# RMSNorm sums as four 32-column products, roots on 128 partitions, and a spread by row-picking products, in a two-layer diffusion backbone

## The chip, the cores and the metric

One core of one Trainium2 chip runs the whole program. TensorE (PE) multiplies, VectorE (DVE), ScalarE (ACT) and GpSimd (POOL) work on elements, and SyncE (SP) starts the DMAs. Each engine takes its own instructions in order and waits on semaphores for the others. The metric is device microseconds of one execution, as the median over runs.

## The reference, cut to what matters

Two layers over 512 latent tokens of width 1024 with 256 context tokens: layer 0 mixes tokens by multi-head latent attention, layer 1 by a Hyena long convolution, and a gated ConvFFN follows each. Every sub-layer begins with an RMS norm and a modulation. The change touches only how the norms are computed:

```python
def rmsnorm(x, g):
    y = x * lax.rsqrt(jnp.mean(x * x, axis=-1, keepdims=True) + EPS)
    return y * g

hx = modulate(rmsnorm(x, norm_mix_g[i]), sh1, sc1)          # also on the context in layer 0
cq = rmsnorm(h @ w_dq, g_q)                                 # width 512
ckv = rmsnorm(kv[..., :KV_LORA], g_kv)                      # width 256
x = x + g1 * mixer(hx)
x = x + g2 * conv_ffn(modulate(rmsnorm(x, norm_ffn_g[i]), sh2, sc2))
return rmsnorm(x, final_g)
```

## The kernel before, in words

Activations lie with the width on partitions and tokens along the free dimension, so the sum over the width is a sum over partitions, and it is made on TensorE. The weights of the large products are split in a high and a low part (`wh`, cast on ACT, L137; `wl`, a subtraction on DVE, L138), and so are the activations (`hxh`/`hxl`, `hf0h`/`hf0l`, `hf1h`/`hf1l`, ...): a product is three matmuls. All matmuls are issued through one helper, so they share line L68.

A norm (class `Norm`, L240 to L304) goes through these steps. Chunk by chunk of 128 channels, ACT squares into `sqa` (the first chunk) or into `sq` (L273), and POOL adds `sq` into `sqa` (L275); the last chunk is squared on DVE into its own `sq` (L280). `colsum` multiplies `sqa` and the last `sq` with a column of ones: 128 tokens of squares are the stationary operand, the moving operand has one column, and the sums land in `cols`, one token per partition, one column for each 128 tokens. `finish` takes the reciprocal root on DVE by a bit trick and three Newton steps (11 instructions on `rsq`, 128 partitions by 2, 4 or 6 columns), makes diagonal matrices `dg` (the identity times a column of roots, L301), and a product of `ones` with `dg` spreads the roots over all partitions (`bc`, `bcc`, `bk`, `bq` in PSUM). `modulated` (L312) then scales on DVE (`hx`, L314), casts on ACT (`...h`, L315) and subtracts on DVE (`...l`, L316).

Norms stand in these places, in order of time: the latent input (4 blocks of 128 tokens, `x`), whose squares are made during the filter phase; the context input (2 blocks, `xc`); `nk` (6 blocks, width 256, spread into `bk`); `nq` (4 blocks, width 512, spread into `bq`); then four norms in two halves of 256 tokens each: before the first FFN (`hf0`), before Hyena (`hy`), before the second FFN (`hf1`) and the final one.

The filter phase (before 73 us) makes the Hyena filters: TensorE makes `fps`, DVE multiplies by a window into `ff` (the window `win` is from ACT), ACT and POOL or DVE split `ff` into `pqh` and `pql`, TensorE transforms these to `fa`, `fb`, `fo`, and DVE evaluates (`fee`, `fev`, `fs`). Between these products stand those of the modulation vectors (class `Mods`): `modp` is four products of 32 stationary columns each that fill four quarters of the PSUM partitions, ACT copies it to `ev` (in the tag "sq"), `modq` transposes it, DVE adds the bias into `modc`. After layer 0's start the modulation is summed on DVE instead (`macc`, L227).

The order on each engine comes from a list scheduler that places every instruction by its dependences and its free buffers; buffers come from pools in which a tag has a fixed number (`bufs`) that are reused in turn. The tag "sq" has two.

Of the kernel before, what the change touches and what calls it, by code (L numbers as in the profile page):

```python
# [44 lines left out]
    VOFF[_n] = (_o, _w)  # L45
    _o += _w
NV = _o
CST = [("ident", 128), ("perm", 128), ("tneg", 4), ("sgn", 1)]
COFF = {}
_o = 0  # L50
for _n, _w in CST:
    COFF[_n] = (_o, _w)
    _o += _w
NCST = _o


@with_exitstack
def hybrid_kernel(ctx, tc, A, out):
# [35 lines left out]
        psum[:] = [stack.enter_context(tc.tile_pool(name=name, bufs=1, space=PSUM, reuse_waits="tile")), n, o]  # L94

    vec = gp.tile([P, NV], F32, name="vec")
    cst = gp.tile([P, NCST], F32, name="cst")
    dma(out=cst, in_=A["cst"])
    dma(out=vec, in_=A["vec"])

    def V(name, a=0, b=None):
# [3 lines left out]
    def K(name):  # L105
        o, w = COFF[name]
        return cst[:, o:o + w]
# [2 lines left out]
    ident_r = gp.tile([P, P], F32R, name="ident_r")  # L110
    perm_r = gp.tile([P, P], F32R, name="perm_r")
    nc.vector.tensor_copy(out=ident_r, in_=ident)
    nc.vector.tensor_copy(out=perm_r, in_=K("perm"))
    ones = gp.tile([P, P], F32, name="ones")
    nc.gpsimd.memset(ones, 1.0)
    modc = gp.tile([P, 2, 48, 2], F32, name="modc")
    gsc = gp.tile([P, 5, 8], F32, name="gsc")
    hcc = gp.tile([P, 3, 24], F32, name="hcc")
    sc = gp.tile([P, 8, 32], F32, name="sc")
    nc.gpsimd.memset(sc, 0.0)  # L120
    act(out=sc[:, :, 0], in_=V("c"), func=AF.Silu)
    act(out=sc[:, :, 1], in_=V("cctx"), func=AF.Silu)

    fspec = dr.tile([4, 2, P, 2, 2, 256], F32, name="fspec")
    xspill = dr.tile([P, NC, T], F32, name="xspill")
# [33 lines left out]
    class Mods:  # L159
# [31 lines left out]
        def step_pe(self, n, ws, pool, ahead=0):  # L191
            for _ in range(min(n, len(self.todo))):
                l, u, n, k = self.todo.pop(0)
                self.rows(sc[:, k, :], ws.pop(0), n, k == 0, k == NC - 1)
                if k == NC - 1:
                    self.columns(l, u, n, 2, pool)
                if ahead and len(self.todo) >= ahead:
                    ws.append(self.load(self.todo[ahead - 1], pool, "mw", ahead))
# [15 lines left out]
        def step(self, n, pool, bufs, after):  # L214
            self.age += 1
            self.finish()
            if self.age > 1:
                self.flush()
            for _ in range(min(n, len(self.todo))):
                k0 = self.todo.pop(0)  # L220
                l, u, n, k = k0
                w = self.load(k0, pool, "mw", bufs)
                if k == 0:
                    self.acc = pool.tile([P, 2048], F32, tag="macc", name="macc", bufs=2)[:, :n * 1024]
                    i = vts(out=self.acc, in0=w, scalar1=sc[:, k, 0:1], scalar2=None, op0=ALU.mult)
                else:
                    i = stt(out=self.acc, in0=w, scalar=sc[:, k, 0:1], in1=self.acc, op0=ALU.mult, op1=ALU.add)  # L227
                in_order(after, i)
                if k == NC - 1:
                    self.due = (self.acc, l, u, n, pool)  # L230
                    self.age = 0
# [8 lines left out]
    class Norm:  # L240
        def __init__(self, n, nt, dim, tmp, halves=1):
# [4 lines left out]
            self.due, self.n_add = [], 0  # L246
            self.cols = [pso("cols") for _ in range(halves)]

        def flush(self, lag=0):
            while self.due and self.due[0][0] <= self.n_add - lag:  # L250
                self.colsum(*self.due.pop(0)[1:])

        def colsum(self, src, h, first, last):
            for t in range(self.nth):
                m = mm(self.cols[h][:, t:t + 1], lhsT=src[:, t * P:(t + 1) * P], rhs=ones[:, 0:1],
                       start=first and t == 0, stop=last and t == self.nth - 1)
                self.last[h] = in_order(self.last[h], m)

        def add(self, xj, h=None):
            self.n_add += 1  # L260
            self.flush(self.nh)
            n, w = self.n, self.nth * P
            hs = list(range(self.nh)) if h is None else [h]
            j = self.j[hs[0]]
            for i in hs:
                self.j[i] += 1
            if j == 0 and n > 2:
                self.acc = self.tmp.tile([P, self.nt * P], F32, tag="sqa", name="sqa", bufs=1)
                act(out=self.acc, in_=xj, func=AF.Square)
                return  # L270
            sq = self.tmp.tile([P, self.nt * P], F32, tag="sq", name="sq", bufs=2)[:, :w * len(hs)]
            if j < n - 1 and n > 2:
                act(out=sq, in_=xj, func=AF.Square)  # L273
                acc = self.acc[:, hs[0] * w:hs[-1] * w + w]
                nc.gpsimd.tensor_tensor(out=acc, in0=acc, in1=sq, op=ALU.add)  # L275
                if j == n - 2:
                    for i in hs:
                        self.due.append((self.n_add, self.acc[:, i * w:(i + 1) * w], i, True, False))
                return
            vtt(out=sq, in0=xj, in1=xj, op=ALU.mult)  # L280
            for i, q in enumerate(hs):
                self.due.append((self.n_add, sq[:, i * w:(i + 1) * w], q, j == 0, j == n - 1))

        def finish(self, bc, h=0, after=None, mm_after=None):
            if mm_after is not None:
                self.last = [mm_after] * self.nh
            self.flush()
            nt, tmp = self.nth, self.tmp
            v = tmp.tile([P, 3, 8], F32, tag="rsq", name="rsq", bufs=2)
            vv, y, t_ = v[:, 0, :nt], v[:, 1, :nt], v[:, 2, :nt]  # L290
            in_order(after, vts(out=vv, in0=self.cols[h][:, :nt], scalar1=1.0 / self.dim, scalar2=EPS, op0=ALU.mult,
                                op1=ALU.add))
            vts(out=y.bitcast(I32), in0=vv.bitcast(I32), scalar1=-0.5, scalar2=float(0x5F3759DF), op0=ALU.mult,
                op1=ALU.add)
            for _ in range(3):
                stt(out=t_, in0=y, scalar=-0.5, in1=y, op0=ALU.mult, op1=ALU.mult)
                vtt(out=t_, in0=t_, in1=vv, op=ALU.mult)
                stt(out=y, in0=t_, scalar=1.5, in1=y, op0=ALU.add, op1=ALU.mult)
            dg = tmp.tile([P, self.nt * P], F32, tag="sq", name="dg", bufs=2)
            for t in range(nt):  # L300
                vts(out=dg[:, t * P:(t + 1) * P], in0=ident, scalar1=y[:, t:t + 1], scalar2=None, op0=ALU.mult)  # L301
            n = nt * P // len(bc)
            for i, b in enumerate(bc):
                in_order(mm_after, mm(b, lhsT=ones, rhs=dg[:, i * n:(i + 1) * n], start=True, stop=True))  # L304

    def rstd_bc(chunks, nt, dim, tmp, bc, after=None):
        nm = Norm(len(chunks), nt, dim, tmp)
# [168 lines left out]
    def mla():  # L476
        L = {}
        with ExitStack() as st:
            a1 = st.enter_context(tc.tile_pool(name="a1", bufs=1, side="left"))
            x = a1.tile([P, NC, T], F32, tag="x", name="x")  # L480
            xc = a1.tile([P, NC, TC], F32, tag="xc", name="xc")
            psum_pool(st, "pa", 5)
            mods = Mods([(0, 0, 2), (0, 2, 2)])

# [10 lines left out]
            def first_loads():  # L495
                ws.extend(mods.load(mods.todo[k], *slots[k]) for k in range(NE, 4))
                for i in range(4):
                    dma(out=x[:, 2 * i:2 * i + 2, :], in_=A["x"][:, 2 * i:2 * i + 2, :])
                ws.extend(mods.load(mods.todo[k], *slots[k]) for k in range(4, 8))
                dma(out=xc, in_=A["ctx"])  # L500

            nm = Norm(NC, 4, D, a1)
            hooks, started, wk = [], [], []
# [34 lines left out]
    def latents(step, nm, nrm, a1, a2, x, xc, L):  # L538
# [15 lines left out]
        for rh, rl, n, o in ((hh, hl, T, TC), (ch, cl, TC, 0)):  # L554
# [10 lines left out]
            else:  # L565
                nc.scalar.copy(out=kpe[64:96, :TC], in_=pss[2][64:96, :n])
            step(2)
        nk = Norm(2, 6, 256, nrm)

        def norm_kv(m):  # L570
# [7 lines left out]
        for b in range(2):  # L578
            w = split_w(A["wdq"][b], 2048)
            w = (wcols(w[0], 8, 256), wcols(w[1], 8, 256))  # L580
            pss = [pst(f"dq{i}") for i in range(2)]
            gemm([(pss[0], *w, 0), (pss[1], *w, P)], lambda k: hh[:, k, :], lambda k: hl[:, k, :], 8,
                 halfway=norm_kv if b else None)
            for i in range(2):
                nc.scalar.copy(out=cq[:, 2 * b + i, :], in_=pss[i])
            if b == 0:
                for j in range(2):
                    nk.add(ckv[:, j, :])
            step(2)
        L["wuk"] = split_w(A["wuk"], 2048)  # L590
        wr = wp.tile([P, 2048], F32, tag="wr", name="wr", bufs=3)
# [24 lines left out]
        nq = Norm(4, 4, 512, nrm)  # L616
        for j in range(4):
            nq.add(cq[:, j, :])
        kb = L["kb"]
        kh, kl = kb[0]  # L620
        nc.scalar.copy(out=kh[64:96], in_=kpe[64:96])
        nc.gpsimd.tensor_tensor(out=kl[64:96], in0=kpe[64:96], in1=kh[64:96], op=ALU.subtract)
# [501 lines left out]
    psum_pool(ctx, "pc", 5)  # L1124
    with tc.tile_pool(name="f0", bufs=1, side="left", reuse_waits="tile") as fp:
        x = fp.tile([P, NC, T], F32, name="x0")
        dma(out=x, in_=A["x"])
        mods = Mods([(0, 4, 1)])
        th = ToH(x, Norm(NC, 4, D, fp, 2), 2, 0, 3, fp, "hf0")
# [14 lines left out]
    yh, yl = hyena(hh, hl)  # L1144
    with tc.tile_pool(name="f1", bufs=1, side="left", reuse_waits="tile") as fp:
        x = fp.tile([P, NC, T], F32, name="x1")
        for i in range(4):
            dma(out=x[:, 2 * i:2 * i + 2, :], in_=xspill[:, 2 * i:2 * i + 2, :])
        th = ToH(x, Norm(NC, 4, D, fp, 2), 3, 1, 3, fp, "hf1")
# [145 lines left out]
```

## Time and profile before

| | |
|---|---|
| time, median of 3 runs | 1453.72 us (1452.2 to 1455.11) |
| the profiled execution | 1458.08 us, its span 1456.3 us |
| TensorE | 1385.1 us busy, 95% of the span |
| VectorE | 959.1 us, 66% |
| ScalarE | 562.2 us, 39% |
| GpSimd | 224.2 us, 15% |
| TensorE clock granted, mean | 0.984 of full |

The span is the time between the first and the last instruction that the profiler saw; the execution's own time has 1.8 us more around it. A group of matmuls ends in the profile where its last modelled end lies, so that neighbouring rows overlap; the distance from start to start is what a piece of work takes.

### The profile page before, as it was taken

Reading aid. Unit: us, or ns where it says so; the run is one execution under the profiler, and the core shown is the slowest. Engines: PE = TensorE matmul, PEld = TensorE weight load, DVE = VectorE, ACT = ScalarE, POOL = GpSimd, SP = SyncE. Lnnn points to the kernel's source line nnn. Section 1 sums busy time; section 2 is a strip of 40 time slices with the busy share of each in tenths; the row PEclk is TensorE's granted clock in tenths of the full one; section 3 lists DMA queues with packets and bytes.
Section 4 is the critical chain, followed back from the end, with each engine's and each line's share of the span. In section 5 each row is a group of like instructions: output and inputs, shape, how many; then the busy total and the mean of one; then the engine's idle time right before and its main releaser. Section 6 shows DMA issues by size and latency. Waiting matters only on the chain. (4 is left out here: it accounts for less than half of the span.)

```text
span 1456.3 us, 17263 instructions
## 1 busy us (share of the span) xinstructions
PE 1385.1 (95%) x6702; PEld 1093.2 (75%) x6702; DVE 959.1 (66%) x1493; ACT 562.2 (39%) x853; POOL 224.2 (15%) x188
## 2 busy tenths in 40 slices
PE   5899899999999999999999999999999999999997
PEld 2577765656588878787878987887798888888886
DVE  6875665567377877567774688988776653355545
ACT  5444454546434433123432343323334432234421
POOL 4401054335330000000001103331300000000011
PEclk9999999999998999999999999999999999999998
DMA  9672511113262754765523442222313222332121
GB/s 372 215 270 98 145 41 48 43 64 115 80 232 85 240 174 151 260 228 174 183 70 137 141 164 88 87 87 68 136 59 116 78 74 100 115 112 78 60 80 59
DMA packets 46670, 186.58 MB, mean 128 GB/s; under 512 B 5320, under 2 KB 17864, under 8 KB 32380
## 3 DMA queue, kind: packets, MB, share of 16 engines
q1 hardware_dynamic: 46588, 185.48, 36.7%
q8 instruction: 53, 0.87, 0.2%
q14 instruction: 29, 0.24, 0.0%
HBM read 171.29 MB, written 11.60 MB: 126 GB/s over the span
## 5 line engine op out<-in xcount | busy, mean ns | idle before, releaser
L137 ACT CAST wh<-wr 128x1024 fp32r<-128x1024 f32 (+2 forms) x209 | 195.1, 955 | 190.2 <-PE dn L68 89.0
L138 DVE TENSOR_TENSOR wl<-wr,wh 128x1024 fp32r<-128x1024 f32 (+2 forms) x209 | 246.7, 1196 | 26.4 <-ACT wh L137 24.0
L275 POOL TENSOR_TENSOR sqa<-sqa,sq 128x512 f32<-128x512 f32 (+1 forms) x42 | 57.2, 1361 | 845.8 <-ACT sq L273 844.9
L68 PE MATMUL dn<-gh,wh 128*128 128x512 f32 (+1 forms) x396 | 147.5, 374 | 0.0
L68 PE MATMUL dn<-gl,wh 128*128 128x512 f32 (+1 forms) x396 | 146.4, 370 | 0.0
L68 PE MATMUL dn<-gh,wl 128*128 128x512 f32 (+1 forms) x396 | 146.2, 369 | 0.0
L326 DVE SCALAR_TENSOR_TENSOR z<-ua,vec,z 128x511 f32<-128x511 f32 x44 | 33.0, 750 | 111.3 <-ACT z L325 111.2
L954 DVE SCALAR_TENSOR_TENSOR x<-dn,modc,x 128x512 f32<-128x512 f32 (+1 forms) x36 | 24.9, 691 | 109.1 <-PE dn L68 109.1
L325 ACT ACTIVATE z<-ua,vec 128x512 f32<-128x512 f32 x44 | 34.2, 778 | 150.6 <-PE ua L68 150.6
L68 PEld LDWEIGHTS dn<-gh,wh 128*128 128x128 f32 x396 | 74.4, 188 | 15.6 <-ACT wh L137 0.8
L68 PEld LDWEIGHTS dn<-gh,wl 128*128 128x128 f32 x396 | 74.5, 188 | 14.3
L68 PEld LDWEIGHTS dn<-gl,wh 128*128 128x128 f32 x396 | 74.4, 188 | 13.9
L68 PE MATMUL hz<-hyh,wh 128*128 128x512 f32 (+1 forms) x224 | 82.2, 368 | 0.0
L68 PE MATMUL hz<-hyh,wl 128*128 128x512 f32 (+1 forms) x224 | 81.9, 367 | 0.0
L761 POOL TENSOR_TENSOR acc<-acc,pf 128x512 f32<-128x512 f32 x60 | 76.7, 1299 | 33.1 <-ACT pf L751 32.2
L68 PE MATMUL hz<-hyl,wh 128*128 128x512 f32 (+1 forms) x224 | 81.7, 366 | 0.0
L751 ACT ACTIVATE pf<-s 128x512 f32<-128x512 f32 x96 | 56.9, 596 | 47.6 <-PE s L68 45.2
L68 PE MATMUL ua<-hf1h,wh 128*128 128x512 f32 (+1 forms) x192 | 72.8, 379 | 1.1 <-ACT hf1h L315 1.1
L68 PE MATMUL ua<-hf0h,wh 128*128 128x512 f32 (+1 forms) x192 | 73.5, 383 | 0.0
L68 PE MATMUL ua<-hf1l,wh 128*128 128x512 f32 (+1 forms) x192 | 73.0, 380 | 0.5 <-DVE hf1l L316 0.5
L68 PE MATMUL ua<-hf0l,wh 128*128 128x512 f32 (+1 forms) x192 | 73.2, 381 | 0.0
L68 PE MATMUL ug<-hf0l,wh 128*128 128x512 f32 (+1 forms) x192 | 73.2, 381 | 0.0
(380 smaller groups left out, 3382.6 us busy)
## 6 DMA issues: line engine op xcount, KB each, us to landing
wr<-in_wup SPq DMA_DIRECT2D x44, 1024.0 KB
mw<-in_modw SPq DMA_DIRECT2D x40, 1024.0 KB
wr<-in_wdn SPq DMA_DIRECT2D x32, 704.0 KB
wr<-in_win SPq DMA_DIRECT2D x12, 1024.0 KB
mw<-in_modw SPq DMA_DIRECT2D x16, 512.0 KB
fspec<-fs SPq DMA_DIRECT2D x16, 256.0 KB
wr<-in_wo SPq DMA_DIRECT2D x4, 1024.0 KB
fq<-fspec SPq DMA_DIRECT2D x8, 512.0 KB
```

The lines of the kernel that those rows point to most:

```text
L68: i = nc.tensor.matmul(*args, **kw)
L137: nc.scalar.copy(out=wh[:, c], in_=wr[:, c])
L138: vtt(out=wl[:, c], in0=wr[:, c], in1=wh[:, c], op=ALU.subtract)
L275: nc.gpsimd.tensor_tensor(out=acc, in0=acc, in1=sq, op=ALU.add)
L325: act(out=z, in_=p, func=AF.Identity, bias=b, scale=w1)
L326: stt(out=z[:, 1:T], in0=p[:, 0:T - 1], scalar=w0, in1=z[:, 1:T], op0=ALU.mult, op1=ALU.add)
L751: act(out=pf, in_=s, func=AF.Exp, scale=ATT_SCALE)
L761: add(out=accs[h], in0=prev, in1=pf, op=ALU.add)
L954: i = stt(out=x[:, q, c], in0=job[0][:, c], scalar=mcol(l, 5, q), in1=x[:, q, c], op0=ALU.mult, op1=ALU.add)
```

## The change

Ones become the stationary operand, 32 columns of them, and the squares stream past. A norm of 4 blocks has its 512 tokens in four quarters of 128; each quarter's product goes to its own 32 PSUM partitions, where the sums stand in 32 equal rows. (A half of 256 tokens has quarters of 64, the context 64, `nk` 192.) So the 11 instructions of the root run on all 128 partitions by 64, 128 or 192 columns. There is no `dg`; instead, `pick[:, g, :]`, a matrix with one row of ones at partition 32g, is the stationary operand of four products that spread quarter g's roots over all partitions. `rsq` moves from a tag of its own into the tag "sq". The squares of `nk` are two tiles, and their sums are issued as soon as the tokens' part is there. The permutation matrix `perm` leaves the block of constants, is loaded on its own after the context into a tile of tag "sq", and is cast on POOL instead of DVE. `pick` is set on POOL in three pools; the vector for the modulation products moves.

```diff
     cst = gp.tile([P, NCP], F32, name="cst")
-    dma(out=cst, in_=A["cst"])
+    dma(out=cst, in_=A["cst"][:, :NCP])
...
-    nc.vector.tensor_copy(out=perm_r, in_=K("perm"))
-    ones = gp.tile([P, P], F32, name="ones")
+    ones = gp.tile([P, 64], F32, name="ones")
     nc.gpsimd.memset(ones, 1.0)
+    pick = {}
+
+    def make_pick(pool):
+        t = pick[0] = pool.tile([P, 4, P], F32, name="pick")
+        nc.gpsimd.memset(t, 0.0)
+        for g in range(4):
+            nc.gpsimd.memset(t[32 * g:32 * g + 1, g, :], 1.0)
...
+        def square(self, name):
+            return self.tmp.tile([P, min(self.nt, 4) * P], F32, tag="sq", name=name, bufs=2)
...
         def colsum(self, src, h, first, last):
-            for t in range(self.nth):
-                m = mm(self.cols[h][:, t:t + 1], lhsT=src[:, t * P:(t + 1) * P], rhs=ones[:, 0:1],
-                       start=first and t == 0, stop=last and t == self.nth - 1)
+            w = self.nth * 32
+            for g in range(4):
+                q = src[g // 2][:, g % 2 * w:(g % 2 + 1) * w] if isinstance(src, list) else src[:, g * w:(g + 1) * w]
+                m = mm(self.cols[h][32 * g:32 * g + 32, :w], lhsT=ones[:, 0:32], rhs=q,
+                       start=first, stop=last)
                 self.last[h] = in_order(self.last[h], m)
...
-            nt, tmp = self.nth, self.tmp
-            v = tmp.tile([P, 3, 8], F32, tag="rsq", name="rsq", bufs=2)
-            vv, y, t_ = v[:, 0, :nt], v[:, 1, :nt], v[:, 2, :nt]
-            in_order(after, vts(out=vv, in0=self.cols[h][:, :nt], scalar1=1.0 / self.dim, scalar2=EPS, op0=ALU.mult,
+            w = self.nth * 32
+            v = self.square("rsq")
+            vv, y = v[:, :w], v[:, w:2 * w]
+            t_ = v[:, 2 * w:3 * w] if w <= P else self.square("rsq2")[:, :w]
+            in_order(after, vts(out=vv, in0=self.cols[h][:, :w], scalar1=1.0 / self.dim, scalar2=EPS, op0=ALU.mult,
                                 op1=ALU.add))
...
-            dg = tmp.tile([P, self.nt * P], F32, tag="sq", name="dg", bufs=2)
-            for t in range(nt):
-                vts(out=dg[:, t * P:(t + 1) * P], in0=ident, scalar1=y[:, t:t + 1], scalar2=None, op0=ALU.mult)
-            n = nt * P // len(bc)
-            for i, b in enumerate(bc):
-                in_order(mm_after, mm(b, lhsT=ones, rhs=dg[:, i * n:(i + 1) * n], start=True, stop=True))
+            n = 4 // len(bc)
+            for g in range(4):
+                b = bc[g // n][:, (g % n) * w:(g % n + 1) * w]
+                in_order(mm_after, mm(b, lhsT=pick[0][:, g, :], rhs=y, start=True, stop=True))
...
                 dma(out=xc, in_=A["ctx"])
+                perm = a1.tile([P, T], F32, tag="sq", name="perm", bufs=2)[:, :P]
+                dma(out=perm, in_=A["cst"][:, NCP:])
+                nc.gpsimd.tensor_copy(out=perm_r, in_=perm)
...
                 for j in range(2):
                     nk.add(ckv[:, j, :])
+                nk.flush()
             step(2)
```

The change also moves instructions on every engine. On ACT in the filter phase, from the first square of the latent input `x` on, before:

```order
L269 ACTIVATE sqa<-x 128x512
L440 CAST pqh<-ff 128x512
L273 ACTIVATE sq<-x 128x512
L433 ACTIVATE win<-dec,cst 128x512
...
L273 ACTIVATE sq<-x 128x512 x2
...
L453 ACTIVATE fee<-fa 128x512
L273 ACTIVATE sq<-x 128x512 x2
L433 ACTIVATE win<-dec,cst 128x512
L440 CAST pqh<-ff 128x512 x2
L433 ACTIVATE win<-dec,cst 128x512
L440 CAST pqh<-ff 128x512 x2
L433 ACTIVATE win<-dec,cst 128x512
L181 COPY ev<-modp 128x512
```

And now, from the same place to the same copy:

```order
L279 ACTIVATE sqa<-x 128x512
...
L470 ACTIVATE fee<-fa 128x512
L457 CAST pqh<-ff 128x512 x2
L450 ACTIVATE win<-dec,cst 128x512
L457 CAST pqh<-ff 128x512 x2
L450 ACTIVATE win<-dec,cst 128x512
L291 ACTIVATE sq<-x 128x512 x6
L186 COPY ev<-modp 128x512
```

The six squares that POOL adds have moved from among the casts to behind the last of these windows and right ahead of `ev`. POOL's six additions move with them, behind all six of its `pql` in this stretch, with the cast of `perm` after the second; the buffers of the first three squares are one and the same, since `perm` holds the other of the tag "sq".

On PE in the second part of the filter phase, before (`hs_...` are the hidden layer's values):

```order
L68 MATMUL cols<-ones,sqa 128x1 x4
...
L68 MATMUL fps<-w3h,hs_148 128x512
L68 MATMUL modp<-mw,sc 32x512 x4
L68 MATMUL fps<-w3l,hs_148 128x512
L68 MATMUL fps<-w3h,hs_149 128x512
L68 MATMUL cols<-ones,sq 128x1 x4
L68 MATMUL modp<-mw,sc 32x512 x8
L184 MATMUL modq<-cst,ev 128x128 x4
L68 MATMUL fps<-w3h,hs_146 128x512
```

And now:

```order
L69 MATMUL fps<-w3h,hs_155 128x512
L69 MATMUL modp<-mw,s_104 32x512 x4
L69 MATMUL fps<-w3l,hs_155 128x512
L69 MATMUL fps<-w3h,hs_156 128x512
L69 MATMUL modp<-mw,s_104 32x512 x8
L69 MATMUL cols<-sqa,ones 32x128 x4
L189 MATMUL modq<-cst,ev 128x128 x4
L69 MATMUL fps<-w3h,hs_153 128x512
```

The sums of `sqa`, which stood some ten products earlier, now stand behind the last `modp` and ahead of `modq` and of the remaining twelve `fps`; the sums of the last `sq` and the spread `bc` come later still.

On DVE at the start of the first FFN, before (the roots of the first half, `rsq`, stand ahead of the last two `macc`):

```order
L298 SCALAR_TENSOR_TENSOR rsq<-rsq 128x2
L227 SCALAR_TENSOR_TENSOR macc<-mw,sc,macc 128x1024
L900 SCALAR_TENSOR_TENSOR x_3361<-pj_3601,modc,x_3361 128x256
L227 SCALAR_TENSOR_TENSOR macc<-mw,sc,macc 128x1024
L138 TENSOR_TENSOR wl<-wr,wh 128x1024
L301 TENSOR_SCALAR dg<-cst,rsq 128x128 x2
L189 TENSOR_TENSOR modc<-modq,vec 128x8
L138 TENSOR_TENSOR wl<-wr,wh 128x1024
L280 TENSOR_TENSOR sq<-x_3361 128x256
L237 SCALAR_TENSOR_TENSOR gsc<-modc,vec 128x8
L314 SCALAR_TENSOR_TENSOR hx<-x_3361,gsc,bc 128x256
```

And now, from the same `macc` on:

```order
L232 SCALAR_TENSOR_TENSOR macc<-mw,sc,macc 128x1024
L927 SCALAR_TENSOR_TENSOR x_3367<-pj_3613,modc,x_3367 128x256
L232 SCALAR_TENSOR_TENSOR macc<-mw,sc,macc 128x1024
L143 TENSOR_TENSOR wl<-wr,wh 128x1024
L310 TENSOR_SCALAR rsq<-cols 128x64
L143 TENSOR_TENSOR wl<-wr,wh 128x1024
L194 TENSOR_TENSOR modc<-modq,vec 128x8
L312 TENSOR_SCALAR rsq<-rsq 128x64
L298 TENSOR_TENSOR sq<-x_3367 128x256
L315 SCALAR_TENSOR_TENSOR rsq<-rsq 128x64
L242 SCALAR_TENSOR_TENSOR gsc<-modc,vec 128x8
L316 TENSOR_TENSOR rsq<-rsq 128x64
```

All eleven instructions of the root have moved behind both `macc` and a `wl`, and nine of them behind `sq`, the square of the second half's last chunk; seven more of them follow before the first `hx`.

## Rows read from the trace of the kernel before

**Rows 1.** The page: engines' busy time, share of the span, instructions.
```profile
PE 1385.1 (95%) x6702; PEld 1093.2 (75%) x6702; DVE 959.1 (66%) x1493; ACT 562.2 (39%) x853; POOL 224.2 (15%) x188
```
**Rows 2.** Timeline, ACT, filter phase: start, duration, line, operation [idle before, releaser].
```profile
32.30 0.63 ACT L273 ACTIVATE sq<-x 128x512 f32<-128x512 f32 x1
...
40.44 0.63 ACT L273 ACTIVATE sq<-x 128x512 f32<-128x512 f32 x1 [1.07 <-POOL sqa L275]
...
49.66 0.72 ACT L433 ACTIVATE win<-dec,cst 128x512 f32<-128x512 f32 x1
```
**Rows 3.** Timeline, POOL, filter phase.
```profile
33.00 1.83 POOL L275 TENSOR_TENSOR sqa<-sqa,sq 128x512 f32<-128x512 f32 x1 [0.64 <-ACT sq L273]
...
36.04 7.10 POOL L275 TENSOR_TENSOR sqa<-sqa,sq 128x512 f32<-128x512 f32 x5
```
**Rows 4.** Timeline, PE, from the filter phase to the first latent product.
```profile
43.87 0.95 PE L68 MATMUL cols<-ones,sqa 128*128 128x1 f32 x8
...
45.80 1.06 PE L68 MATMUL modp<-mw,sc 128*32 128x512 f32 x8
...
48.23 1.92 PE L68 MATMUL modp<-mw,sc 128*32 128x512 f32 x16
50.92 0.66 PE L184 MATMUL modq<-cst,ev 128*128 128x128 f32 x4 [0.76 <-ACT ev L181]
...
60.70 0.74 PE L68 MATMUL fo<-pqh,dfto0h 128*128 128x512 f32 x2 [1.94 <-ACT pqh L440]
63.42 0.80 PE L68 MATMUL fo<-pql,dfto0h 128*128 128x512 f32 x1 [1.98 <-POOL pql L441]
...
74.74 0.50 PE L68 MATMUL kv<-hxh,wh 128*128 128x512 f32 x1 [0.58 <-ACT hxh L315]
```
**Rows 5.** Timeline, DVE, the same stretch.
```profile
48.34 0.16 DVE L291 TENSOR_SCALAR rsq<-cols 128x4 f32<-128x4 f32 x1 [0.52 <-PE cols L68]
...
52.33 0.19 DVE L189 TENSOR_TENSOR modc<-modq,vec 128x32 f32<-128x32 f32 x1
...
54.24 1.28 DVE L466 SCALAR_TENSOR_TENSOR fs<-fo,fev 128x512 f32<-128x512 f32 x2
...
60.67 0.42 DVE L280 TENSOR_TENSOR sq<-xc 128x256 f32<-128x256 f32 x1 [2.59 <-POOL sqa L275]
...
73.11 1.40 DVE L314 SCALAR_TENSOR_TENSOR hx<-x,gsc,bc 128x512 f32<-128x512 f32 x2
```
**Rows 6.** Tile `rsq`, one of its groups: ns minimum/median/maximum, first and last start, forms.
```profile
L296 DVE SCALAR_TENSOR_TENSOR rsq<-rsq x36: 151/161/1145, 49.3 to 1447.1; 128x2 f32<-128x2 f32 x27, 128x4 f32<-128x4 f32 x6, 128x6 f32<-128x6 f32 x3
```
**Rows 7.** Tile `bc`, the final norm's scaling by it, columns as above.
```profile
L1158 DVE SCALAR_TENSOR_TENSOR x<-x,vec,bc x16: 472/475/482, 1440.3 to 1452.3; 128x256 f32<-128x256 f32 x16
```
**Rows 8.** Timeline, PE, context norm, `nk` and `nq`.
```profile
87.34 0.70 PE L68 MATMUL bcc<-dg,ones 128*128 128x256 f32 x2 [0.77 <-DVE dg L301]
...
127.75 1.40 PE L68 MATMUL cols<-ones,sq 128*128 128x1 f32 x12
...
133.10 1.56 PE L68 MATMUL bk<-dg,ones 128*128 128x384 f32 x4 [1.05 <-DVE dg L301]
```
**Rows 9.** Timeline, DVE, start of the first FFN.
```profile
438.13 0.48 DVE L301 TENSOR_SCALAR dg<-cst,rsq 128x128 f32<-128x128 f32 x2
...
440.96 0.42 DVE L280 TENSOR_TENSOR sq<-x 128x256 f32<-128x256 f32 x1 [0.61 <-POOL sqa L275]
...
441.57 0.48 DVE L314 SCALAR_TENSOR_TENSOR hx<-x,gsc,bc 128x256 f32<-128x256 f32 x1
```
**Rows 10.** Timeline, PE, the same place.
```profile
442.71 0.56 PE L68 MATMUL ua<-hf0h,wh 128*128 128x256 f32 x1
```
**Rows 11.** Timeline, PE, start of the second FFN.
```profile
1067.42 0.39 PE L68 MATMUL ua<-hf1h,wh 128*128 128x256 f32 x1 [1.09 <-ACT hf1h L315]
```
**Rows 12.** Timeline, DVE and PE, the final norm's second half.
```profile
1445.57 0.16 DVE L291 TENSOR_SCALAR rsq<-cols 128x2 f32<-128x2 f32 x1 [0.70 <-PE cols L68]
...
1448.34 1.16 PE L68 MATMUL bc<-dg,ones 128*128 128x256 f32 x2 [2.80 <-DVE dg L301]
```

More of the change, by code (lines that the diff above doesn't have):

```diff
@@ L47 @@
 NV = _o
-CST = [("ident", 128), ("perm", 128), ("tneg", 4), ("sgn", 1)]
+CST = [("ident", 128), ("tneg", 4), ("sgn", 1), ("perm", 128)]
 COFF = {}
@@ L54 @@
 NCST = _o
+NCP = COFF["perm"][0]
 @with_exitstack
@@ L96, in hybrid_kernel @@
     vec = gp.tile([P, NV], F32, name="vec")
-    cst = gp.tile([P, NCST], F32, name="cst")
-    dma(out=cst, in_=A["cst"])
+    cst = gp.tile([P, NCP], F32, name="cst")
+    dma(out=cst, in_=A["cst"][:, :NCP])
     dma(out=vec, in_=A["vec"])
@@ L118, in hybrid_kernel @@
     hcc = gp.tile([P, 3, 24], F32, name="hcc")
[L119 to L122, printed above, removed]
+    sc = gp.tile([P, 8], F32, name="sc")
     fspec = dr.tile([4, 2, P, 2, 2, 256], F32, name="fspec")
@@ L193, in step_pe @@
                 l, u, n, k = self.todo.pop(0)
-                self.rows(sc[:, k, :], ws.pop(0), n, k == 0, k == NC - 1)
+                self.rows(pick[1][:, k, :], ws.pop(0), n, k == 0, k == NC - 1)
                 if k == NC - 1:
@@ L224, in step @@
                     self.acc = pool.tile([P, 2048], F32, tag="macc", name="macc", bufs=2)[:, :n * 1024]
-                    i = vts(out=self.acc, in0=w, scalar1=sc[:, k, 0:1], scalar2=None, op0=ALU.mult)
+                    i = vts(out=self.acc, in0=w, scalar1=sc[:, k:k + 1], scalar2=None, op0=ALU.mult)
                 else:
-                    i = stt(out=self.acc, in0=w, scalar=sc[:, k, 0:1], in1=self.acc, op0=ALU.mult, op1=ALU.add)
+                    i = stt(out=self.acc, in0=w, scalar=sc[:, k:k + 1], in1=self.acc, op0=ALU.mult, op1=ALU.add)
                 in_order(after, i)
@@ L270, in add @@
                 return
-            sq = self.tmp.tile([P, self.nt * P], F32, tag="sq", name="sq", bufs=2)[:, :w * len(hs)]
+            if self.nt > 4:
+                w = self.nt * 64
+                sqs = [self.square("sq")[:, :w] for _ in range(2)]
+                for i, t in enumerate(sqs):
+                    c = slice(i * w, i * w + w)
+                    vtt(out=t, in0=xj[:, c], in1=xj[:, c], op=ALU.mult)
+                self.due.append((self.n_add, sqs, 0, j == 0, j == n - 1))
+                return
+            sq = self.square("sq")[:, :w * len(hs)]
             if j < n - 1 and n > 2:
@@ L481, in mla @@
             xc = a1.tile([P, NC, TC], F32, tag="xc", name="xc")
+            s2 = pick[1] = a1.tile([P, 8, 32], F32, name="s2")
+            nc.gpsimd.memset(s2, 0.0)
+            act(out=s2[:, :, 0], in_=V("c"), func=AF.Silu)
+            act(out=s2[:, :, 1], in_=V("cctx"), func=AF.Silu)
+            nc.gpsimd.tensor_copy(out=sc, in_=s2[:, :, 0])
+            make_pick(a1)
             psum_pool(st, "pa", 5)
@@ L567, in latents @@
             step(2)
+        kb = L["kb"]
         nk = Norm(2, 6, 256, nrm)
@@ L618, in latents @@
             nq.add(cq[:, j, :])
-        kb = L["kb"]
         kh, kl = kb[0]
@@ L1126, in hybrid_kernel @@
         x = fp.tile([P, NC, T], F32, name="x0")
+        make_pick(fp)
         dma(out=x, in_=A["x"])
@@ L1146, in hybrid_kernel @@
         x = fp.tile([P, NC, T], F32, name="x1")
+        make_pick(fp)
         for i in range(4):
```

## The prediction

> **What bounds the kernel now.** I read the page first, then the timelines of the stretches in which a norm stands, since the change touches nothing else. The page shows that PE is busy 95% of the span and every other engine far less [rows 1]; so work taken from DVE, ACT or POOL is worth something only where PE waits for it, and work taken from PE is worth its length. The timelines show where PE does wait: in the filter phase, where it waits for splits by ACT and POOL and then for DVE's `hx` [rows 4], and around each spread of roots, where it waits for `dg` [rows 8, 12] or for the activations made with the spread roots [rows 11]. These waits are 0.6 to 2.8 us each. A norm's chain is: last square, column sums, eleven root instructions, `dg`, spread, `hx`, cast, first product.
>
> **Prices.** A root instruction on 2 columns takes 0.16 us and starts 0.196 us after the one before: the last half has eleven of them and two `dg` from 1445.57 to the spread at 1448.34, 2.77 us with `dg` and the handing over [rows 6, 12]. An instruction of the same kind on 256 columns takes 0.475 us [rows 7]. On the straight line between them a column costs 1.24 ns; so 64 columns take 0.24, 128 take 0.32, 192 take 0.40, and with 0.03 between starts eleven are 3.0, 3.8 and 4.7 us. The `dg` go away (2 for a half norm in 0.48 [rows 9]). A half norm's chain on DVE is thus 3.0 against 2.77: slower by 0.2, or by 0.5 where `dg`'s end already stood apart.
>
> Column sums: eight records for two tensors' worth of squares took 0.95, 0.12 each, though only one column streams [rows 4]; that is the load of 128 stationary columns. Now 32 are loaded. The nearest row is `modp`, also four quarters of 32 columns with 512 streaming: 0.13 a record [rows 4]. Ours stream 64 to 192 columns, so a record lies between nothing and 0.13; I take 0.05. A norm of 4 blocks saves about 0.5 of each 0.95, a half 0.2, `nk` 0.9 of each 1.40 [rows 8].
>
> The spread has as many streamed columns as before (four products of 64 are one of 256) but four stationary operands in place of one, at two records each. At least it takes what eight such loads took, 0.95 [rows 4]; at most that and the 0.70 of today's two records [rows 8]. I take 1.1, or +0.4 for each spread.
>
> The row of one `modp` between `fps` (8 records, 1.06) against the two together (16 records, 1.92) leaves at most 0.1 for going into the four quarters and out again [rows 4]. The Trainium skill, "TensorEngine Tiling (Array Packing)", Key Properties, says that changing the tiling mode drains TensorE, which speaks against this change, since it goes in and out at every column sum. By the row about 24 such changes are 2.4 us at most; I take 1 us of it, inside the terms below.
>
> **Term 1, the filter phase.** Before, the six ACT squares lie between 32.30 and 41.1, POOL has added them by 43.1 (36.04 + 7.10), and the sums stand in cover of the `fps` at 43.87 [rows 2 to 4]. Now ACT makes the first after the last window, and PE, in order, meets the sums before `modq` and twelve `fps`. That window ended at 50.4 [rows 2]. Two things ahead of it are gone: the first sums on PE, 0.95 [rows 4], and a root on DVE that waited 0.52 for the second sums ahead of a product with a window [rows 5]; that gives 49.0. Then: the first square, 0.63; six additions at 1.28 to 1.42 each (7.10/5 [rows 3]; 1.83 beside a busy DVE is the upper bound), 8.1; twice POOL waits for a square made into the same buffer, 0.7 each, 1.4; ends at 59.2. The cast of `perm` lies in the second wait. PE reaches the sums at 48.3 (48.23, two sums earlier, plus 1.92, less the 0.95 twice), so it idles for 11 us. `modq` starts at 59.7 after the sums, against 50.92: 8.8 later. What absorbs it? PE then had 1.94, 1.98 and 0.58 of idle before the first `kv` product [rows 4]. If these vanish, the loss is 8.8 − 4.5 = 4.3; that is the lower bound. But `hx` comes from DVE, which is itself held: it runs `modc` at 52.33 and `hx` at 73.11 with 2.59 idle, 18.2 of work [rows 5]. Now two `fs` (1.2) are done ahead, and eleven roots on 128 columns (3.8 less one at its start, 3.5) lie in that row in place of before it; then the spread, 0.8. From `modc` at 60.3: 60.3 + 17.0 + 3.5 + 0.8 = 81.6 for `hx`, against 73.11. **+8.5** (4.3 to 12, the upper end with additions of 1.83 each).
>
> **Term 2, context, `nk`, `nq`.** Four `modp` products move from where they delay `kv` to where PE waits for `hx` anyway, −1.0 [rows 4]; `nk`'s sums are issued ahead of the end of the products and shrink, −1.7 for both sets [rows 8]; the waits of 0.77 and 1.05 for `dg` shrink or are filled by products placed ahead, −0.5; the longer chain of `nq` in front of its first product +1.1 (4.0 and a spread against 3.2), and `nk`'s and the context's spreads, +0.4. Net **−1.7** (−4 to +1).
>
> **Term 3, first FFN.** Before, the roots of the first half were finished while DVE waited for the projection; `hx` began at 441.57, right after the square that waited for POOL (440.96) [rows 9], and the first `ua` at 442.71 [rows 10]. Now nine roots follow that square, with `gsc` among them: 441.35 + 10 × 0.27 = 444.05, then the spread, 0.9, and `hx` at 445.0: **+3.4** (+1, if the scheduler's earlier sums let POOL finish sooner, to +4.5). PE has nothing queued that doesn't need `hf0h`.
>
> **Term 4, the other halves.** Before Hyena and before the second FFN the chain is 0.3 longer and the spread 0.4: 0.7 each, the latter straight into the 1.09 that `ua` waits [rows 11]. At the end of the program nothing covers: sums −0.2, chain +0.2, spread +0.4. Together **+1.8** (0 to +3). The second halves lie beside PE's own work and cost nothing; if that cover were gone, 0.7 each.
>
> Sum: 8.5 − 1.7 + 3.4 + 1.8 = **+12.0**. Against the profiled execution, 1458.08 with a span of 1456.3, that is a span of 1468.3 and about 1470.1; this execution was 4.4 above the median, and the difference carries over: 1453.72 + 12.0 = 1465.7. A change under 0.2%, 2.9 us, could not be told from none by such a measurement.
>
> **Rivals.** *Absorbed.* DVE gets its work done in PE's standstill, and only PE's own row is late: term 1 is 4.3 and term 3 is 1, so 4.3 − 1.7 + 1 + 1.8 = +5.4, 1459.1; the old idle of 4.5 speaks for it, DVE's unbroken row of 17 us against it. *POOL beside DVE.* Each of the six additions takes 1.83 as the one at 33.00 did [rows 3]: +3 on the main case, and with a clock lower after the standstill some 2 more, 1471; DVE standing still meanwhile speaks against it. *The other side: the early sums are not late.* If the squares are done in time, as when ACT reaches them earlier than the order of the splits suggests, PE loses only what POOL ends after 50.92. Then term 1 is near −1 (the first sums' saving), term 3 +1, term 4 +1 and term 2 −4: −3, some 1450.7. It decides at POOL's sixth addition: it must end by 51, 8 us before my reckoning, and six of them in order take 7.7 by themselves, so the first must start by 43; the order of ACT, which has seven casts ahead of it, makes that unlikely. *Drain.* Each change of tiling costs a full product's latency instead of hiding: a `fps` lasts 0.40 while the next starts 0.24 later, so 0.16 twice for 24 sums, +7.7 on the main case, 1473; the row of `modp` speaks against it. This is the Trainium skill's rule named above ("TensorEngine Tiling (Array Packing)", Key Properties).
>
> **Chances.** Main case with its own range of 1461 to 1470: 0.58. Absorbed: 0.18, of which a third within 0.2% of before. POOL slow: 0.08. Drain: 0.05. Other side: 0.11, of which 0.08 is faster by over 0.2%. So faster 0.08, same 0.09, slower 0.83. The range leaves out the other side, and the top of the slow cases: 1456 to 1471.
>
> **What would show it.** In the trace of the changed kernel: PE idle before `cols<-sqa` at about 48, some 11 us, released by POOL's addition; POOL's six additions from 50 to 59; `hx` near 81 and the first `kv` near 83 against 74.74; eleven wide root instructions of 0.32 right ahead of that `hx`; `ua` near 446 less the shift carried from before (it and everything after stand some 7 later); column sums of half norms below 0.4; spreads near 1.1. I am wrong if the squares on ACT begin before 45, if POOL's additions run while PE still has products, or if wide roots take 0.2 rather than 0.3.

## The result, and the profile after

The changed kernel takes 1469.1 us (median of 4 runs, 1464.52 to 1470.8) against 1454.08 of the kernel before beside it (4 runs, 1452.2 to 1455.11): a ratio of 1.010, 95% interval 1.0075 to 1.0125, some 15 us slower. 1465.7 had been forecast, in a range of 1456 to 1471. The profiled execution after is the fastest of its four, 1464.52, and the one before was the slowest of its runs, 1458.08. So the spans of the two traces differ by 6.4 us only, and they can't be subtracted as a whole.

On the page of the changed kernel PE is busy for less time than before [rows 1], while the span is longer:

```profile
PE 1376.8 (94%) x6836; PEld 1082.6 (74%) x6836; DVE 962.8 (66%) x1462; ACT 563.1 (38%) x853; POOL 228.9 (16%) x205
```

The time was lost in the filter phase. The timeline of ACT there (start, duration, operation, idle before and its releaser):

```profile
49.15 0.72 ACT L450 ACTIVATE win<-dec,cst 128x512 f32<-128x512 f32 x1
49.77 0.61 ACT L291 ACTIVATE sq<-x 128x512 f32<-128x512 f32 x1
51.76 0.63 ACT L291 ACTIVATE sq<-x 128x512 f32<-128x512 f32 x1 [1.38 <-POOL sqa L293]
...
60.30 0.59 ACT L186 COPY ev<-modp 128x512 f32<-128x512 f32 x1 [2.56 <-POOL sqa L293]
```

And of POOL:

```profile
50.46 1.26 POOL L293 TENSOR_TENSOR sqa<-sqa,sq 128x512 f32<-128x512 f32 x1 [1.26 <-ACT sq L291]
52.46 1.26 POOL L293 TENSOR_TENSOR sqa<-sqa,sq 128x512 f32<-128x512 f32 x1 [0.74 <-ACT sq L291]
53.67 0.29 POOL L526 CAST perm_r<-perm 128x128 fp32r<-128x128 f32 x1
54.46 5.80 POOL L293 TENSOR_TENSOR sqa<-sqa,sq 128x512 f32<-128x512 f32 x4 [0.51 <-ACT sq L291]
58.50 1.77 POOL L293 TENSOR_TENSOR sqa<-sqa,sq 128x512 f32<-128x512 f32 x1
```

The last row is the last of the four by itself. It runs beside the one square that DVE makes then:

```profile
58.45 0.69 DVE L298 TENSOR_TENSOR sq<-x 128x512 f32<-128x512 f32 x1 [7.29 <-POOL sqa L293]
```

The squares begin after the last window, at 49.8, where they began at 32.3 before [rows 2], and the two engines hand one buffer to and fro. The first of them waits for no buffer and no load: it stands there in ACT's order. POOL ends at 60.26 where it ended at 43.1 [rows 3]. PE's timeline shows who pays for that:

```profile
46.79 1.92 PE L69 MATMUL modp<-mw,s 128*32 128x512 f32 x16
60.32 0.66 PE L69 MATMUL cols<-sqa,ones 128*32 128x128 f32 x8 [11.60 <-POOL sqa L293]
60.93 1.12 PE L189 MATMUL modq<-cst,ev 128*128 128x128 f32 x4
...
80.75 1.06 PE L69 MATMUL modp<-mw,s 128*32 128x512 f32 x8 [1.51 <-DMA mw<-in_modw]
85.37 2.08 PE L69 MATMUL bc<-rsq,pick 128*128 128x128 f32 x8 [3.56 <-DVE rsq L317]
```

PE stands still for 11.6 us. Then DVE carries the delay on to `hx`, as its timeline shows:

```profile
62.09 0.19 DVE L194 TENSOR_TENSOR modc<-modq,vec 128x32 f32<-128x32 f32 x1 [2.94 <-PE modq L189]
...
80.40 0.29 DVE L317 SCALAR_TENSOR_TENSOR rsq<-rsq 128x128 f32<-128x128 f32 x1
82.20 1.29 DVE L483 SCALAR_TENSOR_TENSOR fs<-fo,fev 128x512 f32<-128x512 f32 x2 [1.50 <-DMA fspec<-fs]
...
85.03 0.29 DVE L317 SCALAR_TENSOR_TENSOR rsq<-rsq 128x128 f32<-128x128 f32 x1
87.49 1.40 DVE L331 SCALAR_TENSOR_TENSOR hx<-x,gsc,bc 128x512 f32<-128x512 f32 x2 [2.17 <-PE bc L69]
```

`hx` begins at 87.49 against 73.11 [rows 5], 14.4 later. The other places, as starts of PE's first product of a stage in the five traces that matter (from the timelines; the last row is the span):

| | before | after | own_perm | both_own | roots_early |
|---|---|---|---|---|---|
| `kv`, first latent product | 74.74 | 89.04 | 77.20 | 77.04 | 74.67 |
| `pq`, after `nk` and `nq` | 155.57 | 167.23 | 156.10 | 155.94 | 154.10 |
| `pj`, after attention | 387.62 | 397.75 | 389.62 | 389.64 | 387.76 |
| `ua`, first FFN | 442.71 | 455.55 | 447.43 | 443.15 | 441.26 |
| `hz`, Hyena | 826.76 | 837.77 | 829.53 | 825.83 | 823.75 |
| `pj`, after Hyena | 1001.47 | 1011.44 | 1003.71 | 1000.06 | 998.51 |
| `ua`, second FFN | 1067.42 | 1076.76 | 1069.52 | 1065.82 | 1064.17 |
| span | 1456.3 | 1462.7 | 1457.8 | 1452.4 | 1452.2 |

Read it by differences of neighbours. From `kv` to `pq` the changed kernel needs 78.19 against 80.83: 2.6 less. From `pj` to `ua` it needs 57.80 against 55.09: 2.7 more. The stretch from `pq` to `pj` holds no norm, yet it took 232.1, 230.5, 233.5, 233.7 and 233.7 in these five: a single trace is uncertain by that much in a long stretch, and the terms below are read from the short ones.

### The profile page after: what moved, and what is told of

Same layout as the page of the kernel before. It is cut to its first block, busy times and chain, and to the rows that moved or that the text cites. A ratio compares the mean times of both kernels' runs of the same rounds, so it can differ in the third digit from the quotient of the medians.

```text
span 1462.7 us, 17526 instructions
## 1 busy us (share of the span) xinstructions
PE 1376.8 (94%) x6836; PEld 1082.6 (74%) x6836; DVE 962.8 (66%) x1462; ACT 563.1 (38%) x853; POOL 228.9 (16%) x205
## 5 line engine op out<-in xcount | busy, mean ns | idle before, releaser
L69 PE MATMUL ua<-hf0h,wl 128*128 128x512 f32 (+1 forms) x192 | 72.5, 378 | 0.0
```

Of the source, the lines that this page charges most:

```text
L69: i = nc.tensor.matmul(*args, **kw)
```

## The experiments

All edits are to the changed kernel unless the heading says otherwise, and the kernel before ran beside each.

**Own tile for the permutation matrix (own_perm).**

```diff
-                perm = a1.tile([P, T], F32, tag="sq", name="perm", bufs=2)[:, :P]
+                perm = a1.tile([P, P], F32, name="perm")
```

> The changed kernel with one edit: the permutation matrix gets a tile of its own (128 columns) in place of one of the two tiles of tag sq; everything else stays, narrow products, wide roots, picks. Theory (the borrowed buffer is what puts the six squares behind the windows): PE no longer stands still for 11 us at 48, the first kv product begins near 74.5 (74.74 in the kernel before, 89.0 in the changed one), and the time falls by 12 to 15 us to 1454 to 1457. Rival (roots in tag sq, wide roots and picks are what delays the first norm): kv stays at 85 to 89 and the time at 1466 to 1470.

Measured: 1456.63 (12 runs) against 1457.07 of the kernel before (23 runs), ratio 0.9998, interval 0.9987 to 1.001. One line takes back the whole loss. ACT's timeline of this kernel has the squares among the casts again:

```profile
32.10 0.63 ACT L291 ACTIVATE sq<-x 128x512 f32<-128x512 f32 x1
...
40.26 0.63 ACT L291 ACTIVATE sq<-x 128x512 f32<-128x512 f32 x1 [1.06 <-POOL sqa L293]
```

And PE's has the sums of `sqa` back in cover. It has a new wait of 4.37, for a single root instruction that now stands late (the eleventh, at 71.29, while the tenth ended by 60.3):

```profile
43.78 0.43 PE L69 MATMUL cols<-sqa,ones 128*32 128x128 f32 x8
...
71.61 0.90 PE L69 MATMUL bc<-rsq,pick 128*128 128x128 f32 x4 [4.37 <-DVE rsq L317]
...
77.20 0.50 PE L69 MATMUL kv<-hxh,wh 128*128 128x512 f32 x1 [1.30 <-ACT hxh L332]
```

`kv` came at 77.2, neither the 74.5 of the theory nor the 85 of the rival. The borrowed tile explains 12 of the 14 us; the rest is the late root (roots_early, below).

**The same matrix in the kernel before (before_perm_late).** Norms as before; the load and the cast of `perm` as in the change.

```diff
-    nc.vector.tensor_copy(out=perm_r, in_=K("perm"))
...
                 dma(out=xc, in_=A["ctx"])
+                perm = a1.tile([P, T], F32, tag="sq", name="perm", bufs=2)[:, :P]
+                dma(out=perm, in_=A["cst"][:, NCP:])
+                nc.gpsimd.tensor_copy(out=perm_r, in_=perm)
```

> The kernel BEFORE with only the permutation matrix moved as in the change (loaded after the context into a tile of tag sq, cast on POOL); norms as before. Theory: that alone puts the six squares late, PE stands still for 10 to 12 us near 48, and the time rises by 9 to 15 us to 1463 to 1469. Rival (it takes the wide roots as well): within 3 us of 1454.

Measured: 1475.91 (4 runs), ratio 1.0125, interval 1.0102 to 1.0148: 18 to 19 us slower, more than I expected and more than the whole change. PE's timeline has the same standstill with the old, wide sums behind it:

```profile
60.22 1.87 PE L69 MATMUL cols<-ones,sqa 128*128 128x1 f32 x8 [11.59 <-POOL sqa L275]
```

So the tile alone suffices, and the wide roots aren't needed for it. The first `kv` came at 95.19, some 6 later than in the changed kernel: DVE's square of the context stands ahead of `hx` there and waited 4.29 for POOL.

**Borrowed, but given back early (perm_sq_early).** The tile of tag sq stays, its load and cast stand at the start of the program.

```diff
             make_pick(a1)
+            perm = a1.tile([P, T], F32, tag="sq", name="perm", bufs=2)[:, :P]
+            dma(out=perm, in_=A["cst"][:, NCP:])
+            nc.gpsimd.tensor_copy(out=perm_r, in_=perm)
...
                 dma(out=xc, in_=A["ctx"])
-                perm = a1.tile([P, T], F32, tag="sq", name="perm", bufs=2)[:, :P]
-                dma(out=perm, in_=A["cst"][:, NCP:])
-                nc.gpsimd.tensor_copy(out=perm_r, in_=perm)
```

> The changed kernel, with the permutation matrix still in a tile of tag sq, but loaded and cast at the start of the program in place of after the context. Theory (the harm is that the borrowed tile is given back late): the squares go back among the casts, PE doesn't stand still at 48, kv begins near 77 as with a tile of its own, and the time is 12 to 15 us below that of the changed kernel. Rival (any borrowing of one of two tiles starves the squares): kv at 85 or later.

Measured: 1457.3 (10 runs), ratio 1.0018, interval 1.0003 to 1.0033; the first `kv` at 78.44, the sums of `sqa` at 44.53 without a wait. By the ratios this is 0.8% below the changed kernel, 12 us. So the harm is little in the borrowing (by the ratios 0.2% against own_perm), and nearly all in where the load and the cast stand. In the changed kernel's trace that load itself holds nothing up: SP issues it at 26.29, and the cast at 53.67 waits for no DMA. What came late is the place that the scheduler gave to the squares and the cast when the tile was borrowed late; how it reckoned that is not shown.

**Roots of the half norms out of tag sq (own_roots).**

```diff
-            v = self.square("rsq")
+            v = self.square("rsq") if self.nh == 1 else self.tmp.tile([P, T], F32, tag="sg", name="sg", bufs=2)
```

> The changed kernel with one other edit: in the norms made in two halves the roots lie in the tag sg of the FFN, which is free then, not in tag sq; permutation matrix as in the change. Theory (the buffer, not the width of the roots, moves the roots at the first FFN behind macc and the second square): from the first pj product to the first ua the time falls by 2 to 3.5 us to that of the kernel before (55.1), and the whole by as much, to 1465.5 to 1467. Rival (wide roots and four-part spread cost it): that stretch stays at 57.8 and the time at 1469.

Measured: 1464.06 (4 runs), ratio 1.0048, interval 1.0029 to 1.0067. In the trace `pj` to the first `ua` takes 53.5 (397.47 to 450.98), against 57.8 in the changed kernel and 55.1 before: 4.3 less, more than expected. By the ratios the whole is 0.5% or 7.5 us under the changed kernel, with some 4.6 of uncertainty. In the changed kernel's timeline of DVE the chain stands behind the second half's square and ends in a spread that waits:

```profile
449.77 0.42 DVE L298 TENSOR_TENSOR sq<-x 128x256 f32<-128x256 f32 x1
450.12 0.22 DVE L315 SCALAR_TENSOR_TENSOR rsq<-rsq 128x64 f32<-128x64 f32 x1
...
452.19 0.23 DVE L317 SCALAR_TENSOR_TENSOR rsq<-rsq 128x64 f32<-128x64 f32 x1
454.48 0.87 DVE L331 SCALAR_TENSOR_TENSOR hx<-x,gsc,bc 128x256 f32<-128x256 f32 x2 [2.06 <-PE bc L69]
```

In this kernel's it stands ahead of the last `macc`, and `hx` waits for nothing but DVE's own row:

```profile
444.86 0.22 DVE L317 SCALAR_TENSOR_TENSOR sg<-sg 128x64 f32<-128x64 f32 x1
...
449.90 0.48 DVE L331 SCALAR_TENSOR_TENSOR hx<-x,gsc,bc 128x256 f32<-128x256 f32 x1
```

**The kernel before with its narrow roots in tag sq (before_roots_sq).**

```diff
-            v = tmp.tile([P, 3, 8], F32, tag="rsq", name="rsq", bufs=2)
+            v = (tmp.tile([P, 3, 8], F32, tag="rsq", name="rsq", bufs=2) if self.nh == 1 else
+                 tmp.tile([P, T], F32, tag="sq", name="rsq", bufs=2)[:, :24].rearrange("p (a b) -> p a b", b=8))
```

> The kernel BEFORE with one edit: the roots of the half norms, still 128 by 2, take a tile of tag sq. Theory (the tile, not the width, moves the roots at the first FFN behind macc): from the first pj product to the first ua 56.5 to 58.5 us against 55.1, the time 1 to 4 us above that of the kernel before. Rival (narrow roots keep their place): 55.1, no change.

Measured: 1457.67 (10 runs), ratio 1.0018, interval 1.0003 to 1.0033. `pj` (388.07) to `ua` (445.44) takes 57.4, 2.3 more than before: the tile moves the roots, whatever their width.

**Both (both_own).** The edits of own_perm and own_roots together.

> Both edits together: the change without the two borrowed buffers. Theory: the narrow column sums and the earlier nk sums are worth 2 to 4 us once nothing is late, 1450 to 1452.5, faster than the kernel before (1454.1). Rival (going in and out of the four-quarter mode and the longer root chain eat it): 1454 or more.

Measured: 1453.29 (12 runs) against 1457.07, ratio 0.998, interval 0.9967 to 0.9992. This is what the change is worth without its two borrowed tiles: about 0.2% faster, 3 to 4 us under the kernel beside it, which itself ran 3 us above the 1454.1 that the expectation started from. The rival that going in and out of the four quarters or the longer chain eats all of it falls. In this kernel's timeline of PE, around a pair of sums in a row of equal products:

```profile
815.13 0.28 PE L69 MATMUL dn<-gh,wl 128*128 128x256 f32 x1
815.34 0.32 PE L69 MATMUL cols<-sqa,ones 128*32 128x64 f32 x8
815.47 0.29 PE L69 MATMUL cols<-sq,ones 128*32 128x64 f32 x8
815.70 0.38 PE L69 MATMUL dn<-gh,wh 128*128 128x256 f32 x1
```

A `dn` starts every 0.12 here, so two sums, with the gaps on entering and leaving the four quarters, cost 0.57 − 0.12 = 0.45. In the timeline of the kernel before, the same pair of old sums costs 0.92 − 0.12 = 0.80:

```profile
816.44 0.28 PE L68 MATMUL dn<-gh,wl 128*128 128x256 f32 x1
816.55 0.50 PE L68 MATMUL cols<-ones,sqa 128*128 128x1 f32 x4
816.92 0.58 PE L68 MATMUL cols<-ones,sq 128*128 128x1 f32 x4
817.36 0.37 PE L68 MATMUL dn<-gh,wh 128*128 128x256 f32 x1
```

**The first norm's roots written down earlier (roots_early).** On top of both edits; the roots are emitted inside the filter phase.

```diff
+            def roots():
+                L["bc"] = [pso("bc")]
+                nm.finish(L["bc"])
...
+                    hooks.extend([()] * 0 + [(roots,)])
...
         to_x = ToH(x, nm, 0, 0, 0, a2, "hx")
+        to_x.bc = L["bc"]
```

> The kernel with both edits (own tile for the permutation matrix, roots of the half norms in tag sg), and one more: the first norm's roots are written down inside the filter phase, ahead of its last products, so that the last of the eleven root instructions stands among the filters' work and not right ahead of hx. In the kernel with both edits the spread of the first norm waited 4.33 us for that one instruction, and the first kv product began at 77.0 against 74.74 in the kernel before the change. Theory (its place, not its width, delays hx): kv begins at 74 to 75 and the time falls by 2 to 2.5 us below that of the kernel with both edits, 0.3% or more below the kernel before. Rival (DVE's row is full anyway): kv stays at 76.5 to 77.

Measured: 1451.47 (12 runs) against 1454.35 (31 runs), ratio 0.9975, interval 0.9959 to 0.999. `kv` came at 74.67, as the theory said. The time is 0.25% below the kernel before, where 0.3% or more was expected. This is the lowest ratio of all, faster than both kernels; against both_own the gain of the trace, 2.4 us at `kv`, is not separated by the intervals.

**Every spread twice (spread_twice).** On top of both edits.

```diff
-                in_order(mm_after, mm(b, lhsT=pick[0][:, g, :], rhs=y, start=True, stop=True))
+                for _ in range(2):
+                    in_order(mm_after, mm(b, lhsT=pick[0][:, g, :], rhs=y, start=True, stop=True))
```

> The kernel with both edits, and every spread product issued twice (the second overwrites the first; 12 spreads, 48 products more). Theory (a spread costs PE its whole length everywhere, since PE is the bound): about 0.8 to 1.0 us for each of 12, 9 to 13 us above the kernel with both edits. Rival (only the spreads that something waits for count, some six): 4 to 6 us.

Measured: 1465.89 (6 runs), ratio 1.0083, interval 1.0055 to 1.011, where both_own had 0.998 in another set of runs: 1.03% or 15 us between them, with some 4 us of uncertainty. The rival of 4 to 6 us falls: spreads behind other products are charged too (from `pj` to the second `ua` 67.53 against 65.76 in both_own). But not each one is: from `pj` to the first `ua` this kernel took 53.50 against 53.51. In PE's timeline the second copy fills waits there, first in both_own, then here:

```profile
437.30 1.10 PE L69 MATMUL bc<-sg,pick 128*128 128x64 f32 x8 [0.36 <-DVE sg L317]
438.89 0.64 PE L69 MATMUL modp<-macc,ones 128*32 128x256 f32 x8 [0.48 <-DVE macc L232]
...
443.63 2.00 PE L69 MATMUL bc<-sg,pick 128*128 128x64 f32 x16 [0.36 <-DVE sg L317]
445.56 0.64 PE L69 MATMUL modp<-macc,ones 128*32 128x256 f32 x8
```

That the middle lies above 12 spreads by 1.0 is not settled.

A spread by products over 32 partitions each wasn't tried; what it would cost, no run here shows.

## Why the prediction was right, and where its terms were off

**Term 1** was right in mechanism. The order alone, which put the squares behind the windows, and the price of POOL's additions (1.28 to 1.42 each; measured 1.26 alone, 1.45 in the mean of the last four) gave the standstill to within 0.6 (11 forecast, 11.6 measured; POOL done at 59.2 forecast, 60.26 measured). Its size was off: +14.3 at `kv` in place of +8.5, and beyond the upper bound of 12. Three things that I had not counted follow the standstill. `modc` came at 62.09, not 60.3. The spread of the first norm took 2.08 in place of 0.8, at half the clock. And DVE waited 1.50 for a store, PE 1.51 for a load. `modc`'s 1.8, the spread's 1.3, DVE's 1.50 and another 0.81 for which DVE waited on the late `fps` at 63.37 make 5.4 of the 5.9 by which `hx` came later than reckoned (87.49 against 81.6). SP explains the waits for the store and the load: in its timeline for the changed kernel the third `mw` load stands there until 75, and the eight stores of `fs` are queued behind it:

```profile
53.09 22.07 SPq L173 DMA_DIRECT2D mw<-in_modw  x3
75.45 9.25 SPq L485 DMA_DIRECT2D fspec<-fs  x8
```

The waits of SP's queue in that stretch (waited for, us in total, times, longest) say for what:

```profile
SPq L173 <- PE modp L69: 15.7, 1, 15.7
```

Before, those stores began at 66.93. I had counted DVE's row as unbroken work, and had not looked at what a late PE does to the queue that empties DVE's buffers. That is the step that was mis-sized: 8.5 forecast for `hx`, 14.4 measured. Its cause, the borrowed tile, I had named in the order's description but not priced apart; own_perm and before_perm_late show that it alone makes the standstill.

**Term 2**, −1.7, measured −2.6 from `kv` to `pq`. The eight 192-column records of `nk`'s first sums took 0.53 (a start at 131.80), against 1.40 [rows 8], 0.07 a record where I took 0.05. But the −2.6 is not the sums' alone: before_perm_late, with the old sums behind the same standstill, took 78.31 there, and roots_early, whose `kv` is as early as before, 79.43, which is 1.4 less than before.

**Term 3**, +3.4, measured +2.7. The roots did move behind the square, and nine of them took 2.3 (2.7 reckoned, with `gsc`). The spread took 1.97 in place of 0.9, but the square came 1.3 earlier after `pj` than in the kernel before.

**Term 4**, +1.8, was wrong in sign. From the first `dn` of the first FFN (570.90 before, 582.49 after) to Hyena's first `hz` the changed kernel needed 0.6 less; from `pj` to the second `ua` 65.32 against 65.95; and the end took 6.03 from the last `dn` to the scaling of `x` against 5.92. The first of these is long but repeats: 255.9 to 256.2 in the three traces with the old norms, 255.3 to 255.7 in the six with the new ones and single spreads. The longer chain and spread are there, but I priced only the waits, and not what the norms' own products take of PE beside other products. Each pair of the half norms' sums saves 0.35 there, and the spread takes as much back. PE's timeline around the spread of Hyena's second half, before and after:

```profile
834.54 0.28 PE L68 MATMUL hz<-hyl,wh 128*128 128x256 f32 x1
834.67 0.67 PE L68 MATMUL bc<-dg,ones 128*128 128x256 f32 x2
...
835.30 0.28 PE L68 MATMUL hz<-hyh,wh 128*128 128x256 f32 x1
...
845.03 0.28 PE L69 MATMUL hz<-hyl,wh 128*128 128x256 f32 x1
845.15 1.00 PE L69 MATMUL bc<-rsq,pick 128*128 128x64 f32 x8
...
846.16 0.28 PE L69 MATMUL hz<-hyh,wh 128*128 128x256 f32 x1
```

Less two `hz` of 0.12 each, the spread takes 0.76 − 0.24 = 0.52 there before and 1.13 − 0.24 = 0.89 after. So the sums don't explain the sign by themselves; why these stretches became shorter is open.

**Sum.** From these stretches: 14.3 − 2.6 + 2.7 − 0.6 − 0.6 + 0.1 = 13.3; the runs gave 15 with an interval from 11 to 18. Forecast were 12.0. The stretches left out, which are long, make −6.9 between these two traces (6.4 in the spans). One of them repeats too: from the first to the last `dn` of the second FFN it is 249.0 to 249.2 in the three traces with the old norms and 247.6 to 248.1 in the six with the new, some −1.3, with no cause shown. So the single terms are no surer than a microsecond or two. That the total came so near was partly luck, by errors of opposite sign: term 1 too low by 5.8, term 4 too high by 2.9.

**The rivals.** *Absorbed* (1459.1) fell: PE's waits for splits and filters shrank (1.94 and 1.98 before, 0.74 and 0.37 now), but DVE set the pace, and PE waited 3.56 for its roots. *POOL beside DVE* fell: the last addition, beside DVE's square, took 1.77, but the first, beside DVE's `fs`, took 1.26, and the other four, with DVE standing still, 1.26 to 1.35 each. *Drain* fell as a price: the trace of both_own has a gap of about 0.1 on either side of a pair of sums, and both sums with their gaps are cheaper than the old ones. The prediction's bound for it was read too low: one `modp` against two leaves 2 × 1.06 − 1.92 = 0.20 for going in and out, not 0.1. The Trainium skill, "TensorEngine Tiling (Array Packing)", Key Properties, says that changing the tiling mode drains TensorE; whether that gap is the drain, no run here shows. *The other side* needed POOL to be done by 51; it was done at 60. With its own tile for `perm`, POOL is done by 43 again, and that kernel equals the one before; without either borrowed tile it is 0.2% faster.

## What to carry to other kernels

A tile borrowed from a rotating tag costs little by its size and much by when it is given back: here 128 columns of a constant, loaded behind the context and cast late, cost more than 11 us, while the edits to the arithmetic made the kernel 0.2% faster. Compare the instruction order before the durations, and when an in-order engine is found late, follow it into the DMA queue and the other engines' buffers as well. Where one engine is the bound, price each of its own instructions at every place, and see whether it falls into a wait there or not.

## What the runs showed that was not expected

The spread of 64 or 128 columns a quarter takes PE 1.0 to 1.16 us when PE was busy before, and 1.9 to 2.1 in most places where it had waited for 3 us or more: by the windows view of the changed kernel the granted clock is 1.00 from 40 to 48 us, and 0.50 from 85 to 89, which is 1.2 in place of 2.4 GHz, right behind a wait of 3.56 for the roots. The columns here are stretch, length, busy time and number of instructions of PE, PEld, DVE, ACT and POOL, granted clock, share and rate of the DMAs:

```profile
40.00:48.00 8.00, 8.00 (x48) 3.92 (x50) 4.67 (x9) 2.44 (x4) 1.36 (x2) 1.00 0.92 287
...
85.00:89.00 4.00, 2.66 (x24) 2.20 (x24) 1.70 (x3) 0.73 (x2) 0.88 (x1) 0.50 1.06 287
```

Where no other products fill the wait for the roots, a spread's eight records can meet the low clock, as the old two records did at the end of the program (1.16 [rows 12]; granted clock 0.56 from 1448.3 to 1449.5). In own_roots, where products stand right ahead of it, the spread before the first FFN took 1.10; in the changed kernel 1.97:

```profile
452.47 1.97 PE L69 MATMUL bc<-rsq,pick 128*128 128x64 f32 x8 [4.03 <-DVE rsq L317]
```

A wait doesn't bring the low clock each time. The final norm's last spread took 1.94 after a wait of 3.01 in both_own (granted clock 0.50), but 1.14 after one of 3.00 in the changed kernel (0.89 from 1455.0 to 1456.2):

```profile
1455.06 1.14 PE L69 MATMUL bc<-rsq,pick 128*128 128x64 f32 x8 [3.00 <-DVE rsq L317]
```
